# A hybrid attention and retention encoder layer on Trainium2: the gate's totals as split sums, the gate inside the last columns of w_out, and the last rows stored in six pieces

## The chip, the core and the metric

The kernel runs on one core of one Trainium2 chip. The metric is device time in microseconds (us): the median of three runs before the change is 965.22 us (965.08 to 965.33). Engines are named as in the profile: PE multiplies matrices, PEld is its weight load, DVE, ACT and POOL are the vector, scalar and GpSimd engines, SP is the engine that issues most DMA transfers. PE works on two kinds of fp32 here: plain fp32 (`F32`), and `fp32r` (`F32R`), a reduced form that it multiplies faster. The kernel keeps precision by splitting a value into a high part `hi`, rounded to fp32r, and a low part `lo`, the remainder, and by adding the products hi*hi, hi*lo and lo*hi.

## What is computed

One layer for 512 positions (`SEQ`) of width 2048 (`D_MODEL`), one batch. Cut to its core:

```python
def hybrid_layer(x, c_act, g, w_ada, b_ada, w_in, w_out, dec_f, dec_b):
    mod = c_act @ w_ada + b_ada
    shift, scale, gate = jnp.split(mod, 3, axis=-1)
    h = rms_norm(x, g) * (1.0 + scale[:, None]) + shift[:, None]
    proj = jnp.einsum('bsd,df->bsf', h, w_in)
    ...
    y = jnp.concatenate([y_a * jax.nn.silu(z_a), y_r * jax.nn.silu(z_r)], axis=-1)
    out = jnp.einsum('bsf,fd->bsd', y, w_out)
    return x + gate[:, None] * out

def reference(x, c, norm_gain, w_ada, b_ada, w_in, w_out, ret_decay_logit_f, ret_decay_logit_b, final_gain):
    c_act = jax.nn.silu(c)
    h = x
    for layer in range(DEPTH):
        h = hybrid_layer(h, c_act, norm_gain[layer], w_ada[layer], b_ada[layer], w_in[layer],
                         w_out[layer], ret_decay_logit_f[layer], ret_decay_logit_b[layer])
    return rms_norm(h, final_gain)
```

`DEPTH` is 1. `y_a` comes from eight attention heads, `y_r` from four retention heads, whose output is normalised per head. What matters here is the gate: a row of 2048 numbers, `c_act` times the last third of `w_ada` plus a bias. It multiplies each column of the output projection before `x` is added and the final norm is taken.

## The kernel before

**Projection and heads.** The weights `w_in` come by DMA into `raw` tiles. An *item* of a unit is 512 columns of such a tile: `conv` (line 166) splits it, ACT casting it to `whi` (line 173) and DVE subtracting for `wlo` (line 178), and `mm3` (lines 90 and 92) issues the three matmuls for each product. An item is 12 matmuls with 512 moving columns where the weights are the stationary side (units of q and k), and 24 with 256 where they are the moving side (v and z). `whi` and `wlo` have three buffers each (`WB`), and two items are split ahead of the one being multiplied (`LOOK`). Between items, `run_queue` issues what the heads have to do: scores, exponentials, `op` (the product with the values), and for retention a norm (POOL computes `rs`, DVE scales to `yn`) and transposes `tp` of `yn` (line 866). The accumulators of the projection are `pp`.

**The gate row.** `gate_pieces(h)` handles 512 columns of the gate, for h from 0 to 3: `load` brings 128 rows of `w_ada` into `graw`, `add` multiplies them by the entries of `c` on DVE and adds into `gacc` (128 x 512, line 1007), sixteen times. What is left is the sum over the 128 partitions: `total` (line 1015) takes a column of ones as the stationary side and `gacc` as the moving one, in fp32, so that row 0 of `psg` holds the sums; DVE adds the bias, and SP stores the row to `grow_d` in DRAM. All these pieces stand in the list `gate`, and `some_gate` takes one of them, at a rate of 0.9, each time an item of the later units is fed. Behind the sixteen additions of one h stand an empty entry and then `total`.

**The output projection.** `out_items` runs over column groups dg = 0, 1, 2 of 512 columns, then columns 1536 to 1791. For each, `finish` (line 1206) multiplies the accumulated `po` of a row tile by `gbc` (the gate row, read back from `grow_d` to all partitions, line 1209), adds it to the residual `res` (line 1210), sums the squares for the norm, and multiplies by the final gain `fbc` (line 1227). `columns(g)` issues the loads of `gbc`, `res` and `fbc` for a group. The last 256 columns are held back: during dg = 2 and the group behind it, `last_load` brings their weights and splits them into eight pairs of tiles `lhi` and `llo` (lines 1259 and 1260). At the very end, for each of the four row tiles, 48 matmuls with `lhi` and `llo` run, `finish` with slot 4 completes the row's sum of squares (`ms`) and its inverse root `rsf` (on POOL, line 1226), and `store` (line 1229) scales the 2048 columns by `rsf` and stores them in four pieces of 512.

**What sets the order.** The program is written in one thread, and each engine takes its instructions in an order that a scheduler makes out of it; waits between engines are semaphores. The side work (`sides`) is spread over the items of a column group by `run_items`.

Of the kernel before, what the change touches and what calls it, by code (L numbers as in the profile page):

```python
# [10 lines left out]
F32R = mybir.dt.float32r  # L11
I32 = mybir.dt.int32
AF = mybir.ActivationFunctionType
ALU = mybir.AluOpType
# [3 lines left out]
P = 128  # L18
D = 2048
S = 512  # L20
NT = S // P
NK = D // P
# [21 lines left out]
GR = 2  # L44
# [6 lines left out]
def trunk_kernel(ctx, tc, x, c, norm_gain, w_ada, b_ada, w_in, w_out, dec_f, dec_b, final_gain, out):  # L51
    nc = tc.nc
    x2, o2 = x[0], out[0]
    wi, wo, wa = w_in[0], w_out[0], w_ada[0]

    const = ctx.enter_context(tc.tile_pool(name="const", bufs=1))
# [6 lines left out]
    def bank(pool, nm):  # L63
        return pool.tile([P, 512], F32, tag="b", name=nm)
# [3 lines left out]
    def bank4(nm):  # L68
        turn[0] += 1
        return bank(psA if turn[0] % 4 else psM, nm)  # L70

    def f32(ap):
        return ap.bitcast(F32)
# [63 lines left out]
    make_identity(nc, ident)  # L137
    ones = const.tile([P, P], F32, name="ones")
    nc.gpsimd.memset(ones, 1.0)
    mhalf = const.tile([P, 4], F32, name="mhalf")  # L140
    nc.gpsimd.memset(mhalf, -0.5)
    mln2 = const.tile([P, 1], F32, name="mln2")
# [15 lines left out]
    def after(ins, ref):  # L158
        tc.add_manual_dep(
            ins.ins,  # L160
            ref.ins.name,
            mybir.DependencyInfo(mybir.DependencyClass.NoSync, mybir.DependencyReason.DATA),
            reason="after",
        )

    def conv(src, n, pin_low=None):
        hi = wp.tile([P, 512], F32R, tag="whi", name="whi", bufs=WB)
        lo = wp.tile([P, 512], F32R, tag="wlo", name="wlo", bufs=WB)
        dh, dl = hi[:, :n], lo[:, :n]
        if len(src.shape) == 3:  # L170
            dh = dh.rearrange("p (k f) -> p k f", k=src.shape[1])
            dl = dl.rearrange("p (k f) -> p k f", k=src.shape[1])
        c1 = nc.scalar.copy(dh, src)  # L173
        if pin_low is not None:
            pin_low.append(lambda: pin(nc.vector.tensor_tensor(dl, src, f32(dh), op=ALU.subtract)))
            pin(c1)
            return hi, lo
        c2 = nc.vector.tensor_tensor(dl, src, f32(dh), op=ALU.subtract)  # L178
        marks["conv"] = marks.get("conv", 0) + 1
        if marks["conv"] < 3:  # L180
            after(c1, marks["hh"])
            after(c2, marks["hl"])
        return hi, lo
# [739 lines left out]
    for ci, nk in enumerate(CHUNKS):  # L923
# [18 lines left out]
        for u in order:  # L942
# [22 lines left out]
            if u < N_PERSIST:  # L965
                pss = lambda u=u: persist[u]
                start, stop = ci == 0, lastc
            elif u in kept:
                pss = lambda u=u, kept=kept: kept[u]
                start, stop = False, u not in keep_now  # L970
            else:
                pss = lambda: [bank(psA, "pw") for _ in range(2)]
                start, stop = True, u not in keep_now
# [19 lines left out]
    def gate_pieces(h):  # L993
        st = {}
        gs = slice(2 * D + h * 512, 2 * D + (h + 1) * 512)

        def load(kr):
            raws[h * NK + kr] = pools["w"].tile([P, 512], F32, tag="graw", name="graw", bufs=GR)
            nc.sync.dma_start(raws[h * NK + kr], wa[kr * P : (kr + 1) * P, gs])

        def add(kr):
            raw = raws[h * NK + kr]
            if kr == 0:
                st["acc"] = pools["w"].tile([P, 512], F32, tag="gacc", name="gacc", bufs=1)
                nc.vector.tensor_scalar_mul(st["acc"], raw, ct[:, 0:1])
            else:
                nc.vector.scalar_tensor_tensor(  # L1007
                    st["acc"], raw, ct[:, kr : kr + 1], st["acc"], op0=ALU.mult, op1=ALU.add
                )

        def total():
            row = pools["w"].tile([1, 512], F32, tag="grow", name="grow", bufs=1)
            nc.sync.dma_start(row, b_ada[0:1, gs])
            ps = bank4("psg")[0:1, :]
            nc.tensor.matmul(ps, ones[:, 0:1], st["acc"], start=True, stop=True)
            nc.vector.tensor_tensor(row, row, ps, op=ALU.add)
            nc.sync.dma_start(grow_d[0:1, h * 512 : (h + 1) * 512], row)

        return load, add, total

    dramp = ctx.enter_context(tc.tile_pool(name="dramp", bufs=1, space=bass.MemoryType.DRAM))
    grow_d = dramp.tile([1, D], F32, name="grow_d")
    raws = {}
    gate = []
    gp = [gate_pieces(h) for h in range(4)]
    for n in range(4 * NK + GR):

        def step(n=n):
            if n >= GR:
                gp[(n - GR) // NK][1]((n - GR) % NK)  # L1030
            if n < 4 * NK:
                gp[n // NK][0](n % NK)

        gate.append(step)
        if n >= GR and (n - GR) % NK == NK - 1:
            gate.extend([None, gp[(n - GR) // NK][2]])
    gcount = [0]
    n_gate = len(gate)

# [101 lines left out]
    def ysplit(k):  # L1141
        nc.scalar.copy(yh[k], ytiles[k])
        nc.vector.tensor_tensor(yl[k], ytiles[k], f32(yh[k]), op=ALU.subtract)
# [14 lines left out]
    for k in range(NK):  # L1158
        hi = opA.tile([P, S], F32R, name=f"yh{k}")
        lo = opA.tile([P, S], F32R, name=f"yl{k}")  # L1160
# [27 lines left out]
    res = []  # L1188
# [3 lines left out]
    gbc = opB.tile([P, D], F32, name="gbc")  # L1192
    ssf = opB.tile([P, NT, 5], F32, name="ssf")
    sst = opB.tile([P, NT], F32, name="sst")
    rsf = opB.tile([P, NT], F32, name="rsf")

    def columns(g):
        cs = slice(g * 512, (g + 1) * 512)
        fg = final_gain.rearrange("(a d) -> a d", a=1)
        return (  # L1200
            [lambda: nc.sync.dma_start(gbc[:, cs], grow_d[0:1, cs].to_broadcast([P, 512]))]
            + [lambda t=t: nc.sync.dma_start(res[t][:, cs], x2[t * P : (t + 1) * P, cs]) for t in range(NT)]
            + [lambda: nc.sync.dma_start(fbc[:, cs], fg[0:1, cs].to_broadcast([P, 512]))]
        )

    def finish(t, c0, n, ps, slot):
        cs = slice(c0, c0 + n)
        tmp = opB.tile([P, 512], F32, tag="otmp", name="otmp", bufs=2)
        nc.vector.tensor_tensor(tmp[:, :n], ps, gbc[:, cs], op=ALU.mult)
        nc.vector.tensor_tensor(res[t][:, cs], res[t][:, cs], tmp[:, :n], op=ALU.add)  # L1210
        ss = ssf[:, t, slot : slot + 1]
        if slot < 4:
            nc.scalar.activation(tmp[:, :n], res[t][:, cs], AF.Square, accum_out=ss)
        else:
            nc.vector.tensor_tensor_reduce(
                tmp[:, :n], res[t][:, cs], res[t][:, cs], 1.0, 0.0, ALU.mult, ALU.add, ss
            )
        if slot == 3:
            nc.vector.reduce_sum(sst[:, t : t + 1], ssf[:, t, 0:4], axis=AX.X)
            nc.vector.tensor_scalar(sst[:, t : t + 1], sst[:, t : t + 1], 1.0 / D, EPS, op0=ALU.mult, op1=ALU.add)  # L1220
        if slot == 4:
            ms = small.tile([P, 4], F32, tag="ms", name="ms")
            nc.vector.scalar_tensor_tensor(
                ms[:, 0:1], ss, 1.0 / D, sst[:, t : t + 1], op0=ALU.mult, op1=ALU.add
            )
            nc.gpsimd.tensor_tensor(rsf[:, t : t + 1], ms[:, 0:1], mhalf[:, 0:1], op=ALU.pow)
        nc.vector.tensor_tensor(res[t][:, cs], res[t][:, cs], fbc[:, cs], op=ALU.mult)

    def store(t):
        for j in range(4):  # L1230
            v = res[t][:, j * 512 : (j + 1) * 512]
            if j == 1:
                nc.scalar.activation(v, v, AF.Copy, scale=rsf[:, t : t + 1])
            else:
                nc.vector.tensor_scalar_mul(v, v, rsf[:, t : t + 1])
            (nc.scalar if j % 2 else nc.sync).dma_start(o2[t * P : (t + 1) * P, j * 512 : (j + 1) * 512], v)

    def run_items(items, side):
        done = 0
        for n, it in enumerate(items):  # L1240
# [4 lines left out]
            done = upto  # L1245

    side = [lambda k=k: ysplit(k) for k in [*range(ny, NK), 0]] + columns(0)
    def last_load(k, i):
        if i == 0:
            raw = raw_tile()  # L1250
            nc.sync.dma_start(
                raw.rearrange("p (k f) -> p k f", k=4),
                wo[k * P : (k + 4) * P, 1792:2048].rearrange("(k p) f -> p k f", p=P),
            )
            hold_ll["raw"] = raw
        raw = hold_ll["raw"]
        hi = yp.tile([P, 512], F32R, tag="y", name="lhi")
        lo = yp.tile([P, 512], F32R, tag="y", name="llo")
        nc.scalar.copy(hi, raw[:, i * 512 : (i + 1) * 512])
        nc.vector.tensor_tensor(lo, raw[:, i * 512 : (i + 1) * 512], f32(hi), op=ALU.subtract)  # L1260
        keep.append((hi.rearrange("p (k f) -> p k f", k=2), lo.rearrange("p (k f) -> p k f", k=2)))

    keep = []
    hold_ll = {}
    ll = [lambda k=k, i=i: last_load(k, i) for k in range(0, NK, 4) for i in range(2)]
    sides = [side, columns(1) + columns(2), ll[:5] + columns(3), ll[5:]]
    run_items(g0[nf:], sides[0])
    for dg in (1, 2):
        own = (lambda nm: bank(psP, nm)) if dg == 2 else bank4
# [20 lines left out]
    for t in range(NT):  # L1290
        ts = slice(t * P, (t + 1) * P)
        ps = bank(psP, "po")[:, :256]
# [30 lines left out]
```

## Time and profile before

| | |
|---|---|
| median of three runs | 965.22 us (965.08 to 965.33) |
| the profiled execution | 967.67 us |
| its span, first to last instruction | 965.9 us |
| granted PE clock, mean | 0.995 |
| ACT busy | 376.0 us (39%) |
| POOL busy | 12.5 us (1%) |
| DMA | 141.49 MB, 146 GB/s over the span |

The page's second part divides the span into 40 slices and gives each engine's busy share in tenths:

```profile
PE   7999999999999999999999999999999999999996
DVE  4899998949777876665456565745534382545444
ACT  4742425253254655544343232422333272333321
```

PE is full in all but the first and the last slice; DVE is full at the start and half busy later. A row of the timeline gives the start in us, the duration, the engine, the line of the kernel, the operation and its tiles (output <- inputs), the shape, and a count where equal neighbours are put together; in brackets stands how long the engine was idle before it and what released it. Matmuls are pipelined: one starts before the modelled end of the one ahead, so the distance of two starts is what a matmul costs.

### The profile page before, as it was taken

The numbers are of one execution on the slowest core, as the hardware profiler recorded it, in microseconds if no ns is written. First come the engines' busy times: TensorE is split into PE (matmuls) and PEld (weight loads), VectorE is DVE, ScalarE is ACT, GpSimd is POOL, SyncE is SP. The second block draws the span as 40 slices with busy tenths as digits, with TensorE's granted clock in tenths as the row PEclk, the third lists the DMA queues.
The fourth block names the chain that finished last, engine by engine and source line by source line (L and its number), as shares of the span: only waits on it lengthen the run. The fifth ranks groups of instructions, "written<-read, shape, count | busy, mean of one in ns | idle before, by whom it ended". The sixth has DMA issues, their size and how long they took to land.

```text
span 965.9 us, 14382 instructions
## 1 busy us (share of the span) xinstructions
PE 945.4 (98%) x5602; PEld 821.6 (85%) x5602; DVE 614.0 (64%) x1076; ACT 376.0 (39%) x738; POOL 12.5 (1%) x25
## 2 busy tenths in 40 slices
PE   7999999999999999999999999999999999999996
PEld 6787688788888888988997899988899988888896
DVE  4899998949777876665456565745534382545444
ACT  4742425253254655544343232422333272333321
POOL 2000000000000000000000000000000000000001
PEclk9999999999999999999999999999999999999998
DMA  9997798424642222112225515436322147243304
GB/s 329 333 296 239 262 314 289 162 89 128 198 154 66 87 66 66 55 55 88 67 66 175 196 57 190 147 90 202 101 67 89 66 162 274 90 128 131 110 1 174
DMA packets 108947, 141.49 MB, mean 146 GB/s; under 512 B 5656, under 2 KB 78024, under 8 KB 108496
## 3 DMA queue, kind: packets, MB, share of 16 engines
q1 hardware_dynamic: 107200, 135.83, 43.5%
q10 hardware_dynamic: 1584, 4.72, 1.3%
q8 instruction: 44, 0.72, 0.3%
q14 instruction: 23, 0.19, 0.1%
q0 software_dynamic: 96, 0.03, 0.0%
HBM read 136.36 MB, written 4.20 MB: 146 GB/s over the span
## 4 chain that ended last, share of the span: by engine, by line
PE 82%; DMA 7%; DVE 6%; issue 2%; SPq 1%; ACT 1%; POOL 0%; POOLq 0%; DVEq 0%; ACTq 0%
PE pp L92 24%; PE pp L90 12%; PE po L92 12%; PE pw L92 11%; PE po L90 6%; PE pw L90 6%; PE op L92 3%; DMA araw<-in_w_ada_dram 3%; PE sp L92 2%; DMA graw<-in_w_ada_dram 2%; DVE aacc L234 2%; PE op L90 2%; PE tp L782 1%; DVE wlo L178 1%; SPq L117 1%
## 5 line engine op out<-in xcount | busy, mean ns | idle before, releaser
L173 ACT CAST whi<-raw 128x512 fp32r<-128x512 f32 (+1 forms) x289 | 175.1, 606 | 433.5 <-PE pp L92 203.1
L178 DVE TENSOR_TENSOR wlo<-raw,whi 128x512 fp32r<-128x512 f32 (+1 forms) x288 | 193.5, 672 | 208.3 <-ACT whi L173 201.8
L92 PE MATMUL pp<-wlo,hh 128*128 128x256 f32 x576 | 162.3, 282 | 0.5 <-DVE wlo L178 0.4
L90 PE MATMUL pp<-whi,hh 128*128 128x256 f32 x576 | 162.6, 282 | 0.0
L92 PE MATMUL pp<-whi,hl 128*128 128x256 f32 x576 | 161.6, 281 | 0.0
L90 PEld LDWEIGHTS pp<-whi,hh 128*128 128x128 f32 x576 | 108.5, 188 | 2.5 <-ACT sc L851 1.7
L92 PEld LDWEIGHTS pp<-wlo,hh 128*128 128x128 f32 x576 | 108.6, 189 | 1.9 <-DVE wlo L178 0.9
L92 PEld LDWEIGHTS pp<-whi,hl 128*128 128x128 f32 x576 | 108.6, 188 | 0.0
L90 PE MATMUL pw<-hh,whi 128*128 128x512 f32 x256 | 103.5, 404 | 3.6 <-ACT acc L952 1.9
L92 PE MATMUL pw<-hh,wlo 128*128 128x512 f32 x256 | 102.3, 400 | 0.8 <-DVE wlo L178 0.8
L90 PE MATMUL pp<-hh,whi 128*128 128x512 f32 x256 | 102.0, 398 | 0.4 <-DVE kl L682 0.4
L92 PE MATMUL pw<-hl,whi 128*128 128x512 f32 x256 | 102.0, 398 | 0.0
L92 PE MATMUL pp<-hh,wlo 128*128 128x512 f32 x256 | 101.2, 397 | 0.0
L92 PE MATMUL pp<-hl,whi 128*128 128x512 f32 x256 | 101.2, 395 | 0.0
L92 PE MATMUL po<-wlo,yh 128*128 128x512 f32 (+1 forms) x252 | 92.7, 368 | 0.0
L92 PE MATMUL po<-whi,yl 128*128 128x512 f32 (+1 forms) x252 | 92.6, 368 | 0.0
L90 PE MATMUL po<-whi,yh 128*128 128x512 f32 (+1 forms) x252 | 92.6, 367 | 0.0
L234 DVE SCALAR_TENSOR_TENSOR aacc<-araw,ct,aacc 128x512 f32<-128x512 f32 (+2 forms) x75 | 76.0, 1015 | 6.7 <-ACT aacc L230 3.8
L954 DVE TENSOR_TENSOR acc<-acc,pw 128x512 f32<-128x512 f32 x100 | 67.0, 684 | 8.0 <-PE pw L92 7.6
L1007 DVE SCALAR_TENSOR_TENSOR gacc<-graw,ct,gacc 128x512 f32<-128x512 f32 x60 | 45.0, 750 | 40.9 <-DMA graw<-in_w_ada_dram 40.7
L90 PEld LDWEIGHTS pw<-hh,whi 128*128 128x128 f32 x256 | 48.5, 190 | 19.1 <-DVE acc L954 4.9
L90 PEld LDWEIGHTS pp<-hh,whi 128*128 128x128 f32 x256 | 48.1, 188 | 13.4 <-ACT e L727 0.9
(234 smaller groups left out, 1559.3 us busy)
## 6 DMA issues: line engine op xcount, KB each, us to landing
raw<-in_w_in_dram SPq DMA_DIRECT2D x94, 512.0 KB, 3.7
araw<-in_w_ada_dram SPq DMA_DIRECT2D x48, 512.0 KB, 6.7
graw<-in_w_ada_dram SPq DMA_DIRECT2D x64, 256.0 KB, 2.9
raw<-in_w_out_dram SPq DMA_DIRECT2D x32, 512.0 KB, 3.7
raw<-in_w_in_dram SPq DMA_DIRECT2D x16, 384.0 KB, 4.2
araw<-in_w_ada_dram SPq DMA_DIRECT2D x16, 384.0 KB, 4.9
res<-in_x_dram SPq DMA_DIRECT2D x16, 256.0 KB, 6.2
raw<-in_w_in_dram SPq DMA_DIRECT2D x11, 256.0 KB, 5.8
```

Source lines behind the costliest of these rows:

```text
L90: nc.tensor.matmul(o, lh, rh, start=start, stop=False, skip_group_check=True)
L92: nc.tensor.matmul(o, a, b, start=False, stop=stop and b is (rl if swap else rh), skip_group_check=True)
L117: q.dma_start(raw0[b][:, i * 8 : (i + 1) * 8], wa[i * 8 * P : (i + 1) * 8 * P, b * D : b * D + P].rearrange("(a p) f -> p a f", p=P),)
L173: c1 = nc.scalar.copy(dh, src)
L178: c2 = nc.vector.tensor_tensor(dl, src, f32(dh), op=ALU.subtract)
L234: ins = nc.vector.scalar_tensor_tensor(acc[:, :, :n], rv[:, a], ct[:, kr + a : kr + a + 1], acc[:, :, :n], op0=ALU.mult, op1=ALU.add,)
L782: nc.tensor.transpose(tp_[:, j * P : (j + 1) * P], pt[:, j * P : (j + 1) * P], ident)
L954: nc.vector.tensor_tensor(accs[u][i], accs[u][i], ps[i], op=ALU.add)
L1007: nc.vector.scalar_tensor_tensor(st["acc"], raw, ct[:, kr : kr + 1], st["acc"], op0=ALU.mult, op1=ALU.add)
```

## The change

Three parts, in the diff below. First, `parts` splits `gacc` by the same `conv` that splits weights, so in one of its three pairs of buffers, and `total` sums both halves with two fp32r matmuls over `ones_r`, a 128 x 1 column of ones cast once at the start. `parts` is a new entry of the list `gate` in the place that `total` had, and `total` follows one item behind. Second, the gate goes into the last 256 columns of `w_out`: `last_load` multiplies the raw weights in place by `gbc` (line 1275 of the new kernel), 256 columns at a time, before they are split, and `finish` with slot 4 has no product with the gate. The row of `gbc` for those columns is loaded at the end of the side work of dg = 1. Third, `store` works in six pieces of 256, 384, 384, 384, 320 and 320 columns; ACT scales the second and the fifth and issues the fifth, SP issues the other five.

```diff
--- before.py
+++ after.py
@@ -137,6 +137,7 @@
     make_identity(nc, ident)
     ones = const.tile([P, P], F32, name="ones")
     nc.gpsimd.memset(ones, 1.0)
+    ones_r = const.tile([P, 1], F32R, name="ones_r")
     mhalf = const.tile([P, 4], F32, name="mhalf")
     nc.gpsimd.memset(mhalf, -0.5)
     mln2 = const.tile([P, 1], F32, name="mln2")
@@ -1008,18 +1009,23 @@
                     st["acc"], raw, ct[:, kr : kr + 1], st["acc"], op0=ALU.mult, op1=ALU.add
                 )
 
+        def parts():
+            st["parts"] = conv(st["acc"], 512)
+
         def total():
             row = pools["w"].tile([1, 512], F32, tag="grow", name="grow", bufs=1)
             nc.sync.dma_start(row, b_ada[0:1, gs])
             ps = bank4("psg")[0:1, :]
-            nc.tensor.matmul(ps, ones[:, 0:1], st["acc"], start=True, stop=True)
+            for i in range(2):
+                nc.tensor.matmul(ps, ones_r, st["parts"][i], start=i == 0, stop=i == 1)
             nc.vector.tensor_tensor(row, row, ps, op=ALU.add)
             nc.sync.dma_start(grow_d[0:1, h * 512 : (h + 1) * 512], row)
 
-        return load, add, total
+        return load, add, parts, total
 
     dramp = ctx.enter_context(tc.tile_pool(name="dramp", bufs=1, space=bass.MemoryType.DRAM))
     grow_d = dramp.tile([1, D], F32, name="grow_d")
+    nc.scalar.copy(ones_r, ones[:, 0:1])
     raws = {}
     gate = []
     gp = [gate_pieces(h) for h in range(4)]
@@ -1033,7 +1039,7 @@
 
         gate.append(step)
         if n >= GR and (n - GR) % NK == NK - 1:
-            gate.extend([None, gp[(n - GR) // NK][2]])
+            gate.extend([None, gp[(n - GR) // NK][2], gp[(n - GR) // NK][3]])
     gcount = [0]
     n_gate = len(gate)
 
@@ -1194,11 +1200,15 @@
     sst = opB.tile([P, NT], F32, name="sst")
     rsf = opB.tile([P, NT], F32, name="rsf")
 
+    def gate_row(s):
+        nc.sync.dma_start(gbc[:, s], grow_d[0:1, s].to_broadcast([P, s.stop - s.start]))
+
     def columns(g):
         cs = slice(g * 512, (g + 1) * 512)
+        gs = slice(g * 512, 1792 if g == 3 else (g + 1) * 512)
         fg = final_gain.rearrange("(a d) -> a d", a=1)
         return (
-            [lambda: nc.sync.dma_start(gbc[:, cs], grow_d[0:1, cs].to_broadcast([P, 512]))]
+            [lambda: gate_row(gs)]
             + [lambda t=t: nc.sync.dma_start(res[t][:, cs], x2[t * P : (t + 1) * P, cs]) for t in range(NT)]
             + [lambda: nc.sync.dma_start(fbc[:, cs], fg[0:1, cs].to_broadcast([P, 512]))]
         )
@@ -1206,8 +1216,10 @@
     def finish(t, c0, n, ps, slot):
         cs = slice(c0, c0 + n)
         tmp = opB.tile([P, 512], F32, tag="otmp", name="otmp", bufs=2)
-        nc.vector.tensor_tensor(tmp[:, :n], ps, gbc[:, cs], op=ALU.mult)
-        nc.vector.tensor_tensor(res[t][:, cs], res[t][:, cs], tmp[:, :n], op=ALU.add)
+        if slot < 4:
+            nc.vector.tensor_tensor(tmp[:, :n], ps, gbc[:, cs], op=ALU.mult)
+            ps = tmp[:, :n]
+        nc.vector.tensor_tensor(res[t][:, cs], res[t][:, cs], ps, op=ALU.add)
         ss = ssf[:, t, slot : slot + 1]
         if slot < 4:
             nc.scalar.activation(tmp[:, :n], res[t][:, cs], AF.Square, accum_out=ss)
@@ -1227,13 +1239,14 @@
         nc.vector.tensor_tensor(res[t][:, cs], res[t][:, cs], fbc[:, cs], op=ALU.mult)
 
     def store(t):
-        for j in range(4):
-            v = res[t][:, j * 512 : (j + 1) * 512]
-            if j == 1:
+        cuts = (0, 256, 640, 1024, 1408, 1728, D)
+        for i in range(6):
+            v = res[t][:, cuts[i] : cuts[i + 1]]
+            if i in (1, 4):
                 nc.scalar.activation(v, v, AF.Copy, scale=rsf[:, t : t + 1])
             else:
                 nc.vector.tensor_scalar_mul(v, v, rsf[:, t : t + 1])
-            (nc.scalar if j % 2 else nc.sync).dma_start(o2[t * P : (t + 1) * P, j * 512 : (j + 1) * 512], v)
+            (nc.scalar if i == 4 else nc.sync).dma_start(o2[t * P : (t + 1) * P, cuts[i] : cuts[i + 1]], v)
 
     def run_items(items, side):
         done = 0
@@ -1256,14 +1269,18 @@
         raw = hold_ll["raw"]
         hi = yp.tile([P, 512], F32R, tag="y", name="lhi")
         lo = yp.tile([P, 512], F32R, tag="y", name="llo")
-        nc.scalar.copy(hi, raw[:, i * 512 : (i + 1) * 512])
-        nc.vector.tensor_tensor(lo, raw[:, i * 512 : (i + 1) * 512], f32(hi), op=ALU.subtract)
+        w = raw[:, i * 512 : (i + 1) * 512]
+        for j in range(2):
+            v = w[:, j * 256 : (j + 1) * 256]
+            nc.vector.tensor_tensor(v, v, gbc[:, 1792:2048], op=ALU.mult)
+        nc.scalar.copy(hi, w)
+        nc.vector.tensor_tensor(lo, w, f32(hi), op=ALU.subtract)
         keep.append((hi.rearrange("p (k f) -> p k f", k=2), lo.rearrange("p (k f) -> p k f", k=2)))
 
     keep = []
     hold_ll = {}
     ll = [lambda k=k, i=i: last_load(k, i) for k in range(0, NK, 4) for i in range(2)]
-    sides = [side, columns(1) + columns(2), ll[:5] + columns(3), ll[5:]]
+    sides = [side, columns(1) + columns(2) + [lambda: gate_row(slice(1792, D))], ll[:5] + columns(3), ll[5:]]
     run_items(g0[nf:], sides[0])
     for dg in (1, 2):
         own = (lambda nm: bank(psP, nm)) if dg == 2 else bank4
```

The new lines move instructions on the engines at three places.

**PE, at the second total.** The names: `op` is the product of retention head 0, `pp` with `whi` and `wlo` the projection items behind it. Before:

```order
L90 MATMUL op<-vh_5040,pth 128x256
L92 MATMUL op<-vl_5042,pth 128x256
L92 MATMUL op<-vh_5040,ptl 128x256
L1015 MATMUL psg<-gacc,ones 1x512
L90 MATMUL pp<-whi,hh_85 128x256
L92 MATMUL pp<-wlo,hh_85 128x256
L92 MATMUL pp<-whi,hl_1731 128x256
```

After, at the same place, the projection items follow the `op` matmuls directly:

```order
L90 MATMUL op<-vh_5042,pth 128x256
L92 MATMUL op<-vl_5044,pth 128x256
L92 MATMUL op<-vh_5042,ptl 128x256
L90 MATMUL pp<-whi,hh_85 128x256
L92 MATMUL pp<-wlo,hh_85 128x256
L92 MATMUL pp<-whi,hl_1732 128x256
```

and the total stands further on:

```order
L92 MATMUL pp<-whi,hl_1732 128x256
L90 MATMUL pp<-whi,hh_88 128x256
L92 MATMUL pp<-wlo,hh_88 128x256
L92 MATMUL pp<-whi,hl_1732 128x256
L1020 MATMUL psg<-whi,ones_r 1x512
L1020 MATMUL psg<-wlo,ones_r 1x512
L90 MATMUL pp<-whi,hh_89 128x256
L92 MATMUL pp<-wlo,hh_89 128x256
```

The total moved past two rounds of 24 projection matmuls and the eight transposes `tp` between them, and is two matmuls now. The other three totals moved back by one, three and four items.

**ACT, at the first total.** Here `g` and `e` belong to the gating by SiLU of the first retention unit, and `whi<-raw` is the split of weights. Before:

```order
L725 ACTIVATE g_5105<-pp,mln_137 128x512
L726 ACTIVATE e<-pp 128x512
L727 ACTIVATE e<-e 128x512
L725 ACTIVATE g_5112<-pp,mln_137 128x512
L173 CAST whi<-raw 128x512
L726 ACTIVATE e<-pp 128x512
L727 ACTIVATE e<-e 128x512
L173 CAST whi<-raw 128x512 x7
```

After:

```order
L726 ACTIVATE g_5107<-pp,mln_138 128x512
L727 ACTIVATE e<-pp 128x512
L728 ACTIVATE e<-e 128x512
L726 ACTIVATE g_5114<-pp,mln_138 128x512
L174 CAST whi<-gacc 128x512
L727 ACTIVATE e<-pp 128x512
L728 ACTIVATE e<-e 128x512
L174 CAST whi<-raw 128x512 x8
```

The cast of `gacc` took the place of a weight cast, and that weight cast stands with the others behind the two exponentials.

**DVE, in the output projection.** The place is the end of group dg = 1, when `finish` runs for its four row tiles (lines 1209, 1210, 1227 before; 1220, 1222, 1239 after) while the first pieces of the last columns are split (`llo`) along with the weights of the running group (`wlo`). Before:

```order
L1227 TENSOR_TENSOR res_7877<-res_7877,fbc 128x512
L1209 TENSOR_TENSOR otmp<-po,gbc 128x512 x2
L1210 TENSOR_TENSOR res_7878<-res_7878,otmp 128x512
L178 TENSOR_TENSOR wlo<-raw,whi 128x512
L1210 TENSOR_TENSOR res_7879<-res_7879,otmp 128x512
L1227 TENSOR_TENSOR res_7878<-res_7878,fbc 128x512
L1260 TENSOR_TENSOR llo<-raw,lhi 128x512
L1227 TENSOR_TENSOR res_7879<-res_7879,fbc 128x512
L178 TENSOR_TENSOR wlo<-raw,whi 128x512
L1209 TENSOR_TENSOR otmp<-po,gbc 128x512
L1260 TENSOR_TENSOR llo<-raw,lhi 128x512
```

After:

```order
L1277 TENSOR_TENSOR llo<-raw,lhi 128x512
L1239 TENSOR_TENSOR res_7899<-res_7899,fbc 128x512
L1220 TENSOR_TENSOR otmp<-po,gbc 128x512
L179 TENSOR_TENSOR wlo<-raw,whi 128x512
L1222 TENSOR_TENSOR res_7900<-res_7900,otmp 128x512
L1220 TENSOR_TENSOR otmp<-po,gbc 128x512
L1222 TENSOR_TENSOR res_7901<-res_7901,otmp 128x512
L1275 TENSOR_TENSOR raw<-raw,gbc 128x256 x2
L1239 TENSOR_TENSOR res_7900<-res_7900,fbc 128x512
L1239 TENSOR_TENSOR res_7901<-res_7901,fbc 128x512
L1277 TENSOR_TENSOR llo<-raw,lhi 128x512
L179 TENSOR_TENSOR wlo<-raw,whi 128x512
```

The multiplications of `raw` by `gbc` (line 1275) stand between the rows of `finish`, ahead of the `llo` that needs them, and the `llo` and `wlo` behind them moved back by as many rows.

## The prediction

> **What bounds the kernel now.** First the page's busy shares, then the waits of PE in the stretch 232 to 957 us, behind the opening phase and up to the last matmul.
>
> ```profile
> PE 945.4 (98%) x5602; PEld 821.6 (85%) x5602; DVE 614.0 (64%) x1076; ACT 376.0 (39%) x738; POOL 12.5 (1%) x25
> ```
> ```profile
> PE pp L92 <- DVE wlo L178: 0.4, 1, 0.4
> PE pp L90 <- DVE kl L682: 0.4, 1, 0.4
> ```
>
> PE works nearly all the time, and in 725 us it is seen to wait twice, 0.8 us in all. So up to 957 us the time is the matmuls themselves: an edit counts by the PE time it removes or adds, and by a wait that it makes. Behind the last matmul (957.39) PE is out, and what counts is the chain from there to the last stored byte. The profiled execution took 967.67 us (span 965.9); the sum is made against it and set off against the median, 965.22.
>
> **Gate totals: what goes.** PE's timeline at the first of four totals, and the group of all four:
>
> ```profile
> 507.64 0.28 PE L92 MATMUL pp<-wlo,hh 128*128 128x256 f32 x1
> 507.76 0.28 PE L92 MATMUL pp<-whi,hl 128*128 128x256 f32 x1
> 507.96 1.02 PE L1015 MATMUL psg<-gacc,ones 128*1 128x512 f32 x2
> 508.91 0.49 PE L90 MATMUL pp<-hh,whi 128*128 128x512 f32 x1
> 509.48 0.40 PE L92 MATMUL pp<-hl,whi 128*128 128x512 f32 x1
> 511.35 0.39 PE L92 MATMUL pp<-hl,whi 128*128 128x512 f32 x1
> ```
> ```profile
> L1015 PE MATMUL psg<-gacc,ones x8: 590/591/592, 508.0 to 709.6; 128*1 128x512 f32 x8
> ```
>
> The first number of a row is its start; starts give the pace, since matmuls overlap. A 256-column fp32r matmul starts 0.12 behind the one before (507.64, 507.76). From 509.48 to 511.35 stand eight steps of 512 columns, 0.234 each. From 507.76 to 509.48 there is one step of 256 and two of 512, 0.12 + 0.47 = 0.59 of 1.72 us; the other **1.13 us is the fp32 total**, including its slow start and the stretched matmul behind it. The two fp32r matmuls that replace it have 512 moving columns each. No row shows an fp32r matmul with one output column. The nearest rows are the fp32r ones above, 0.234, and the fp32 total, 1.13; I take 2 x 0.234 = 0.47, since the type is the same and the columns that stream are as many, and keep 1.13 each as the upper end. A total so saves 0.66 to 0.67.
>
> [...]
>
> **The second total also covered a wait.** It stood between the last `op` matmul of retention head 0 and two projection items, into which the transposes `tp` of that head are mixed. Head 1 has the same sequence with no total:
>
> ```profile
> 573.41 0.28 PE L92 MATMUL op<-vh,ptl 128*128 128x256 f32 x1
> 573.62 1.02 PE L1015 MATMUL psg<-gacc,ones 128*1 128x512 f32 x2
> 574.57 0.39 PE L90 MATMUL pp<-whi,hh 128*128 128x256 f32 x1
> 581.36 0.28 PE L90 MATMUL pp<-whi,hh 128*128 128x256 f32 x1
> ```
> ```profile
> 630.68 0.28 PE L92 MATMUL op<-vx,ptl 128*128 128x256 f32 x1
> 633.76 0.83 PE L866 MATMUL tp<-ident,yn 128*128 128x128 f32 x4
> 637.72 0.28 PE L90 MATMUL pp<-whi,hh 128*128 128x256 f32 x1
> ```
> ```profile
> 633.76 0.20 PEld L866 LDWEIGHTS tp<-ident,yn 128*128 128x128 f32 x2 [0.19 <-DVE yn L862]
> ```
>
> From the last `op` to the second item behind (581.36; 637.72 in head 1) it takes 7.95 us with the total and 7.04 without, where the weight load of `tp` waits for `yn`, 0.19 twice. So only 0.91 of the 1.13 goes here: 0.91 - 0.47 = 0.44. The other totals stand beside no such chain. **Sum of the totals: 3 x 0.67 + 0.44 = 2.45 us.**
>
> **What must stay covered.** Each total now first needs a cast of `gacc` on ACT and a subtraction on DVE. It comes as one more item in the row of weight splits and holds one of three pairs of buffers until its matmuls are done; splits of the weights then run one item ahead of PE, not two.
>
> ```profile
> 508.98 0.61 ACT L173 CAST whi<-raw 128x512 fp32r<-128x512 f32 x1
> ```
> ```profile
> L178 DVE TENSOR_TENSOR wlo<-raw,whi 128x512 fp32r<-128x512 f32 (+1 forms) x288 | 193.5, 672 | 208.3 <-ACT whi L173 201.8
> ```
> ```profile
> ACT whi L173 <- PE pp L92: 166.9, 89, 5.0
> ```
>
> The split is 0.61 + 0.67 = 1.3 us, 1.7 with a DVE instruction ahead of it; an item lasts 12 x 0.234 = 2.8 us. ACT's casts waited 166.9 us for PE to free buffers, so there is room. Tightest is the first total: the cast of `gacc` takes the slot of the row at 508.98, the subtraction ends about 510.3, and PE comes to the total one item behind 507.88, at 510.7: 0.4 us to spare. The others have more matmuls in front. I take 0; a miss costs 0.4 or so each, 1 us in all.
>
> **The gate in the last columns' weights.** Sixteen multiplications of 256 columns go to DVE, two ahead of each `lhi` cast, at 0.42 each by the like row L1227, 6.7 us; one product of 256 columns leaves each of the four row tiles.
>
> ```profile
> L1227 DVE TENSOR_TENSOR res<-res,fbc 128x256 f32<-128x256 f32 x8 | 3.3, 417 | 0.0
> ```
> ```profile
> 868.68 0.37 SPq L1251 DMA_DIRECT2D raw<-in_w_out_dram  x1
> 873.16 0.62 ACT L1259 CAST lhi<-raw 128x512 fp32r<-128x512 f32 x1 [0.75 <-DMA raw<-in_w_out_dram]
> 874.44 0.69 DVE L1227 TENSOR_TENSOR res<-res,fbc 128x512 f32<-128x512 f32 x1
> 875.05 0.68 DVE L178 TENSOR_TENSOR wlo<-raw,whi 128x512 fp32r<-128x512 f32 x1
> 878.63 0.39 PE L90 MATMUL po<-whi,yh 128*128 128x512 f32 x1
> ```
>
> They lie beside 92 us of output projection, but in bunches. The tight place is around 870, where `finish` of a column group, two `last_load` pieces and the weight splits share DVE. The split at 875.05 serves the item that PE starts at 878.63: it ends at 875.73, 2.9 us early. After, the load for the third pair of pieces waits longer: its buffer is free only when the second `llo` before it is done, at about 870.8 by the new order on DVE, some 2.1 us later than 868.68. With 4.5 us from there to the data's use (873.16), 875.3, two multiplications (0.7), and two products with `fbc`, `llo` and `wlo` at 0.6 apiece (874.44 to 875.05), the wanted `wlo` ends near 878.4, 0.2 to 0.3 us before PE. I take 0, and up to 1.0 if it is late. What is queued behind a late multiplication on DVE is the next `wlo`, and PE waits for that.
>
> **The tail.** The timeline, the groups, the store's own line and the DMA windows:
>
> ```profile
> 957.71 0.42 DVE L1209 TENSOR_TENSOR otmp<-po,gbc 128x256 f32<-128x256 f32 x1 [2.05 <-PE po L92]
> 958.16 0.42 DVE L1210 TENSOR_TENSOR res<-res,otmp 128x256 f32<-128x256 f32 x1
> 959.33 0.66 POOL L1226 TENSOR_TENSOR rsf<-ms,mhalf 128x1 f32<-128x1 f32 x1 [4.99 <-DVE ms L1223]
> 960.03 0.72 ACT L1233 ACTIVATE res<-res,rsf 128x512 f32<-128x512 f32 x1 [4.93 <-POOL rsf L1226]
> 960.03 1.28 DVE L1235 TENSOR_SCALAR res<-res,rsf 128x512 f32<-128x512 f32 x3 [0.44 <-POOL rsf L1226]
> 960.54 0.81 SPq L1236 DMA_DIRECT2D out_dram<-res  x2
> ```
> ```profile
> L1235 DVE TENSOR_SCALAR res<-res,rsf 128x512 f32<-128x512 f32 x12 | 5.1, 483 | 1.9 <-POOL rsf L1226 1.9
> L355 DVE TENSOR_SCALAR xt<-xt,rsx 128x128 f32<-128x128 f32 x4 | 1.1, 283 | 0.8 <-POOL rsx L351 0.7
> ```
> ```profile
> L1236 SPq DMA_DIRECT2D out_dram<-res x8: 332/366/424, 943.7 to 961.0; - x8
> ```
> ```profile
> 962.00:963.00 1.00, 0.00 (x0) 0.00 (x0) 0.00 (x0) 0.00 (x0) 0.00 (x0) 0.50 0.98 373
> 963.00:964.00 1.00, 0.00 (x0) 0.00 (x0) 0.00 (x0) 0.00 (x0) 0.00 (x0) 0.50 1.02 381
> 964.00:965.00 1.00, 0.00 (x0) 0.00 (x0) 0.00 (x0) 0.00 (x0) 0.00 (x0) 0.50 0.16 57
> ```
>
> The product goes, and the sum reads PSUM itself: 958.16 - 957.71 = **0.45 us**, on the chain to `rsf` and so to the end. Then the store: 1.05 MB leave at some 380 GB/s (the last two columns: share of the DMA engines, GB/s), so the end is the first byte's start plus 2.8 us, as long as pieces are issued fast enough. The first piece has 256 columns in place of 512; its scaling lies between 0.283 (128) and 0.483 (512), 0.35, so its issue comes **0.13 us** earlier. SP issues five pieces at about 0.40 (0.81 for two): 0.40 us at 380 GB/s is 152 KB. The first piece has 131 KB, and SP is 0.06 late behind it; the others have 164 to 196 KB, and SP gets ahead. ACT's first piece (384 columns, under 0.72) is ready before SP comes to it, 0.4 behind the first. Last issue at 1.6 us behind the first, while the data still run: the gain stands. Tail 0.58, between 0.25 (C below) and 0.75 (a start 0.3 earlier, should the small first piece flow at once).
>
> **Sum.** 2.45 + 0.58 = 3.03: 967.67 becomes 964.6, and by the median 965.22 - 3.03 = **962.2 us**.
>
> **Rivals.**
>
> *B, covers torn:* the totals save 2.45, but late splits or DVE around 870 give back 1 to 2 us: 963.2 to 964.2. For it: the margins of 0.3 and 0.4 above; against it: DVE at 64% and ACT's 166.9 us of waiting for PE. 0.17.
>
> *C, store bound by issues:* pieces of 1 to 1.5 KB per partition cannot fill the DMA engines, and the six take longer than the four. If the rate fell from 380 to 340 GB/s, 1.05 MB would take 3.08 for 2.76 us, 0.3 more: tail 0.58 - 0.32 = 0.26, time 962.5. For it: SP's pitch, five issues instead of two; against it: 152 KB per pitch, above. [...] The windows of before (pieces of 2 KB per partition, 373 to 381) can't decide it. 0.13.
>
> *D, slower:* an fp32r matmul with one output column is no faster than fp32. Then each total is two of the old price. With m for one matmul, the change is 8m - 4 x 1.13 + 0.22 - 0.58 (the 0.22 is the wait that the second total covered): at m = 1.13 it gives +4.2, 969.4. It is slower by 0.2% from m = 0.85 on, and within 0.2% from 0.37. [...] This is also the case in which the change does not do what it says. 0.04.
>
> **How the numbers follow.** Forecast 0.66 (961.7 to 962.9), B 0.17, C 0.13, D 0.04. 0.2% of 965.2 is 1.9 us, about what a measurement of this kernel can tell from no change: faster means under 963.3. The forecast and C lie under it, as does a fifth of B: 0.66 + 0.13 + 0.03 = 0.82. Four fifths of B, 0.14, lie within, D above or within: slower 0.03, same 0.15. The range goes from 961.6 (tail 0.75, totals 2.85 if nothing of the covered wait shows and starts are smoother) to 963.8, which takes in C, the forecast and half of B.
>
> **What would show it.** PE's timeline at each total: two matmuls whose starts lie 0.23 apart and no stretched one behind; 1.1 apart would be D. `tp` of head 0 waits 0.2 for `yn`. In PE's waits, rows on `wlo`, `whi` or `psg` above 0.5 in sum would be B, and their times say whether it is a total or 870 to 880. In the tail, the sum at PE's end + 0.3 with no product, the first issue some 0.6 nearer to PE's end, and windows at 370 to 380 GB/s; under 350, or gaps between issues, would be C. A median above 963.3 proves the sum wrong.

## The result and the profile after

The changed kernel takes 953.26 us (median of six, 951.5 to 954.4) against 965.28 before: a ratio of 0.9871, with a 95% interval from 0.9857 to 0.9886. That is **12 us less, four times the 3.0 that was forecast**, and 8 us below the range. The profiled execution after took 951.88 us (span 950.1).

The page's busy line, to be set beside that of before:

```profile
PE 928.7 (98%) x5602; PEld 812.3 (85%) x5602; DVE 619.6 (65%) x1096; ACT 379.0 (40%) x747; POOL 12.5 (1%) x25
```

PE ran as many matmuls as before (5602 in both) and was busy 16.7 us less (945.4 before; the two profiled executions lie 15.8 us apart). No edit takes out that much work, so the step from one matmul to the next must have become shorter. The waits of PE, 225 to 945 us:

```profile
PE pp L92 <- DVE wlo L179: 0.5, 1, 0.5
PE pp L90 <- DVE kl L683: 0.4, 1, 0.4
PE tp L867 <- DVE yn L863: 0.4, 1, 0.4
PE pw L90 <- DVE acc L955: 0.2, 1, 0.2
```

The row of note that is new is the wait for `yn`. It is not the one that the second total used to cover: it lies in the transposes of the last retention head, among matmuls of the output projection, where nothing was forecast. The wait that was forecast shows in the weight loads of head 0 alone, 0.30 and 0.19 for twice 0.19. First the row of the last head, then those of head 0:

```profile
764.22 0.44 PE L867 MATMUL tp<-ident,yn 128*128 128x128 f32 x2 [0.39 <-DVE yn L863]
```
```profile
566.22 0.20 PEld L867 LDWEIGHTS tp<-ident,yn 128*128 128x128 f32 x2 [0.30 <-DVE yn L863]
566.61 0.20 PEld L867 LDWEIGHTS tp<-ident,yn 128*128 128x128 f32 x2 [0.19 <-DVE yn L863]
```

The first total after, in PE's timeline:

```profile
501.65 0.39 PE L92 MATMUL pp<-hl,whi 128*128 128x512 f32 x1
501.88 0.40 PE L92 MATMUL pp<-hh,wlo 128*128 128x512 f32 x1
502.12 0.40 PE L1020 MATMUL psg<-whi,ones_r 128*1 128x512 f32 x1
502.35 0.40 PE L1020 MATMUL psg<-wlo,ones_r 128*1 128x512 f32 x1
502.59 0.39 PE L90 MATMUL pp<-hh,whi 128*128 128x512 f32 x1
```

The two matmuls cost 0.47 us (502.12 to 502.59), with no stretched one behind, just as in the sum. So the totals are not where 12 us came from. The same 48 projection matmuls, which no edit touches, first before, then after (PE's timeline, first and last row of the stretch):

```profile
520.21 0.40 PE L90 MATMUL pp<-hh,whi 128*128 128x512 f32 x1
531.41 0.40 PE L90 MATMUL pp<-hh,whi 128*128 128x512 f32 x1
```
```profile
510.84 0.39 PE L90 MATMUL pp<-hh,whi 128*128 128x512 f32 x1
521.83 0.39 PE L90 MATMUL pp<-hh,whi 128*128 128x512 f32 x1
```

11.20 us before, 10.99 after: 0.2333 and 0.2289 us a step, for the same operands with no wait. To the nanosecond the stretch takes 11.200 and 10.986. Matmuls of 256 columns go from 0.118 to 0.113. **In such stretches a projection matmul costs about 4.4 ns less, whether it streams 512 columns or 256**, and this begins some 35 us after the start, over 450 us ahead of the first total. It isn't so everywhere: the output projection has 0.233, 0.234 before, `op` 0.118 in both, and part of the projection's 256-column stretches stay at 0.118.

The tail did not do what was forecast either. Its timeline after, from the last matmul, with SP's rows one by one, then the DMA windows:

```profile
941.59 0.28 PE L92 MATMUL po<-lhi,yl 128*128 128x256 f32 x1
941.91 0.42 DVE L1222 TENSOR_TENSOR res<-res,po 128x256 f32<-128x256 f32 x1 [2.59 <-PE po L92]
943.07 0.66 POOL L1238 TENSOR_TENSOR rsf<-ms,mhalf 128x1 f32<-128x1 f32 x1 [5.09 <-DVE ms L1235]
943.77 1.31 DVE L1248 TENSOR_SCALAR res<-res,rsf 128x256 f32<-128x256 f32 x4 [0.44 <-POOL rsf L1238]
944.15 0.33 SPq L1249 DMA_DIRECT2D out_dram<-res  x1
...
945.08 0.37 SPq L1249 DMA_DIRECT2D out_dram<-res  x1
945.56 0.39 SPq L1249 DMA_DIRECT2D out_dram<-res  x1
946.37 0.33 SPq L1249 DMA_DIRECT2D out_dram<-res  x1
```
```profile
946.00:947.00 1.00, 0.00 (x0) 0.00 (x0) 0.00 (x0) 0.00 (x0) 0.00 (x0) 0.50 1.00 361
947.00:948.00 1.00, 0.00 (x0) 0.00 (x0) 0.00 (x0) 0.00 (x0) 0.00 (x0) 0.50 0.99 359
```

The first store is issued 2.56 us behind PE's last matmul (944.15 - 941.59), 3.15 before: 0.59 earlier, as forecast. But the span ends 8.51 behind it in both (950.1 - 941.59, 965.9 - 957.39). SP's issues lie 0.5 apart and the fifth 0.81 behind the fourth, at 4.78 and not 4.16; the DMA engines move 360 GB/s, not 380.

### The profile page after: what moved, and what is told of

Same layout as the page of the kernel before. It is cut to its first block, busy times and chain, and to the rows that moved or that the text cites. A ratio compares the mean times of both kernels' runs of the same rounds, so it can differ in the third digit from the quotient of the medians.

```text
span 950.1 us, 14445 instructions
## 1 busy us (share of the span) xinstructions
PE 928.7 (98%) x5602; PEld 812.3 (85%) x5602; DVE 619.6 (65%) x1096; ACT 379.0 (40%) x747; POOL 12.5 (1%) x25
## 4 chain that ended last, share of the span: by engine, by line
PE 81%; DVE 6%; DMA 6%; ACT 2%; issue 2%; SPq 1%; POOL 0%; POOLq 0%; DVEq 0%; ACTq 0%
PE pp L92 23%; PE po L92 12%; PE pp L90 12%; PE pw L92 12%; PE po L90 6%; PE pw L90 6%; PE op L92 3%; DMA graw<-in_w_ada_dram 2%; DMA araw<-in_w_ada_dram 2%; PE sp L92 2%; PE op L90 2%; PE tp L783 1%; DVE wlo L179 1%; DVE aacc L235 1%; SPq L117 1%
```

## The experiments

Two questions: what made untouched matmuls faster, and what ate the tail's 0.59 us? The first clue is what the change does to memory. `ones_r` is allocated among the constants and takes a slot of 32 bytes per partition; every tile that is allocated behind it on the left side stands 32 bytes further on: `raw`, `whi`, `wlo`, the tiles of the heads, `res`. `hh`, `hl`, `yh` and `yl` are allocated from the right side and stay. Before, in the built program, `whi` and `wlo` start at a multiple of 64 bytes and `hh`, `hl` at a multiple plus 32; after, both at a multiple plus 32. (These addresses are the built program's; no trace shows them. The traces show what a shift by 32 or 64 bytes does.) Theory 1: this placement sets the pace. Theory 2: the new instructions and their order do. Theory 3: the executions merely differ.

**Placement alone, and the change without it.** One line for each kernel: in `before_pad32` and `before_pad64` a tile that nothing uses, of 32 or 64 bytes, in the place of `ones_r`; in `after_pad32` 32 bytes more behind `ones_r`; in `after_unshifted` `ones_r` in spare bytes of `mhalf`.

```diff
 # before_pad32 (before_pad64: [P, 16]; after_pad32: the same line in the changed kernel)
+    const.tile([P, 8], F32, name="pad")
     mhalf = const.tile([P, 4], F32, name="mhalf")
```
```diff
 # after_unshifted, against the changed kernel
-    ones_r = const.tile([P, 1], F32R, name="ones_r")
-    mhalf = const.tile([P, 4], F32, name="mhalf")
-    nc.gpsimd.memset(mhalf, -0.5)
+    mhalf = const.tile([P, 8], F32, name="mhalf")
+    ones_r = mhalf[:, 4:5].bitcast(F32R)
+    nc.gpsimd.memset(mhalf[:, 0:4], -0.5)
```

> The kernel before with one unused tile of 32 bytes per partition in the constants' pool, in the place where the change puts ones_r; no instruction differs. Theory 1 (placement: ones_r moves every tile behind it in on-chip memory by 32 bytes, and the pace of the matmuls hangs on that): 953 to 957 us, steps of 0.229 us for 512 columns and 0.113 for 256 in most units, as in the profile after. Theory 2 (the pace follows from the changed instructions, their order or their time): 965, steps of 0.233 and 0.118 as before. Theory 3 (the executions differ for a reason outside the kernel): either, without relation to the pad.

> The kernel before with an unused tile of 64 bytes per partition in the same place. Theory 1, if only the position within 64 bytes counts: 965, as before. If any shift helps: 953 to 957. Theory 2: 965.

> The changed kernel with a further unused 32 bytes behind ones_r, so that all later tiles stand 64 bytes behind their places of before. Theory 1, position within 64 bytes: the pace of before returns, and only the sum of the prediction's terms is left, 961 to 963 us. Theory 2: 953.

> The changed kernel with ones_r in spare bytes of the tile mhalf, so that no other tile moves; the instructions are the same. Theory 1: 962.2 us, 3.0 less than before, the prediction's terms alone, with steps of 0.233 and 0.118. Theory 2: 953, as after.

Measured, with the time of those 48 matmuls in each trace:

| kernel | median us | before, same chip | ratio, 95% interval | 48 matmuls, us |
|---|---|---|---|---|
| before_pad32 | 957.94 | 966.19 | 0.991 [0.9893, 0.9928] | 10.986 |
| before_pad64 | 964.98 | 966.19 | 0.9985 [0.9976, 0.9993] | 11.200 |
| after_pad32 | 963.5 | 966.19 | 0.9973 [0.9962, 0.9984] | 11.199 |
| after_unshifted | 964.02 | 966.19 | 0.9971 [0.9961, 0.9981] | 11.200 |

An unused tile of 32 bytes makes the kernel before 8 us faster, and no instruction differs; 64 bytes do nearly nothing. (The two kernels with `pad32` stand 0.9 and 0.5 us above what was expected of them, on a chip whose kernel before is 0.9 slower than in the section on the result.) The other way round, the changed kernel with its tiles in their old places gains 0.29% (2.8 us by the ratio, 1.8 to 3.8 by its interval; 2.2 between the medians). Theories 2 and 3 fall: the pace follows the bytes in four of four kernels. Its first and last row of the 48 in `before_pad32`:

```profile
513.40 0.39 PE L90 MATMUL pp<-hh,whi 128*128 128x512 f32 x1
524.38 0.39 PE L90 MATMUL pp<-hh,whi 128*128 128x512 f32 x1
```

**Which tiles, and against what?** Only the distance of two operands, or their own place? `before_right32` moves the right side's pools by 32 bytes (a pool of one unused tile opened ahead of `hp`), `before_both32` moves both sides, `before_wp32` moves the weights' pool by 32 and every left-side pool behind it by 64.

```diff
 # before_right32; before_both32 has this and the pad of before_pad32
+    rpad = ctx.enter_context(tc.tile_pool(name="rpad", bufs=1, side="right"))
+    rpad.tile([P, 8], F32, name="padr")
     hp_scope = ExitStack()
```
```diff
 # before_wp32: the pad of before_pad32, and behind the weights' pool
     small = ctx.enter_context(tc.tile_pool(name="small", bufs=8))
+    small.tile([P, 8], F32, name="pads", bufs=1)
```

> The kernel before with 32 unused bytes per partition ahead of the pools on the right side of on-chip memory: hh, hl, yh and yl move by 32 bytes, whi and wlo stay. If the two operands of a matmul must stand alike within 64 bytes (theory 1a, relative): whi at 0 and hh at 0, so the fast steps of 0.229 and 0.113 in the projection, 955 to 959 us. If whi and wlo must stand at 32 (theory 1b, absolute): 965.

> The kernel before with 32 bytes on either side: whi and wlo at 32 within 64 bytes, hh and hl at 0. Theory 1a: they differ again, so the slow steps, 965 us. Theory 1b: 955 to 959.

> The kernel before with 32 bytes ahead of the pool of raw, whi and wlo and 32 behind it, so that all pools behind it (y, the heads' tiles, res) move by 64. If the weights' place against hh and hl is what counts: 955 to 959, as with the pad of 32. If another tile's place does it (those of the heads, of the accumulators, or the engines that write them): 965.

| `whi`, `wlo` within 64 bytes | `hh`, `hl` | kernel | median us | ratio to before | 48 matmuls, us |
|---|---|---|---|---|---|
| 0 | 32 | before | 965.32 | 1 | 11.200 |
| 32 | 32 | before_wp32 | 957.67 | 0.9917 [0.9892, 0.9941] | 10.987 |
| 0 | 0 | before_right32 | 956.06 | 0.9901 [0.9876, 0.9926] | 10.986 |
| 32 | 0 | before_both32 | 965.16 | 0.9998 [0.9984, 1.0011] | 11.200 |

Theory 1a holds and 1b falls: it is the place of the two operands of a matmul **relative to each other**. Alike within 64 bytes, the fast step is there; 32 bytes apart, it is not, in this stretch in all four cells. `before_wp32` shows that the weights against `hh` and `hl` suffice; the tiles of the heads and of `y` keep their places within 64 bytes in it. (`raw` moves with `whi` and `wlo`, but no matmul of the stretch reads it.) First and last row in `before_right32`, then in `before_both32`:

```profile
514.03 0.39 PE L90 MATMUL pp<-hh,whi 128*128 128x512 f32 x1
525.01 0.39 PE L90 MATMUL pp<-hh,whi 128*128 128x512 f32 x1
```
```profile
518.69 0.39 PE L90 MATMUL pp<-hh,whi 128*128 128x512 f32 x1
529.89 0.39 PE L90 MATMUL pp<-hh,whi 128*128 128x512 f32 x1
```

**The tail: six pieces or four?** `after_store4` is the changed kernel with the old `store`; `after_six_alternate` keeps the six pieces and lets SP and ACT issue in turn; `after_five` has pieces of 256, 512, 512, 512, 256.

```diff
 # after_six_alternate
-            (nc.scalar if i == 4 else nc.sync).dma_start(...)
+            (nc.scalar if i % 2 else nc.sync).dma_start(...)
 # after_five: that line, and
-        cuts = (0, 256, 640, 1024, 1408, 1728, D)
-        for i in range(6):
+        cuts = (0, 256, 768, 1280, 1792, D)
+        for i in range(5):
...
-            if i in (1, 4):
+            if i == 1:
```

> The changed kernel with the four pieces of 512 columns of before in store. In the profile after, the last bytes land 7.53 us behind PE's last matmul, 7.47 before, though the first store is issued 0.59 earlier. If the six pieces eat the gain: landing at about 7.0 behind PE's end, 0.5 us less than the changed kernel, 952.8. If the end is set by something else: 7.5, 953.3.

> The changed kernel, its six pieces issued in turn by SP and ACT. If SP's five issues in a row are what makes the six pieces slow: the last bytes land 7.0 to 7.1 us behind PE's end, 7.55 in the changed kernel. If it is the pieces' width (1 to 1.5 KB per partition): still 7.4 or more.

> The changed kernel with five pieces of 256, 512, 512, 512 and 256 columns, issued in turn by SP and ACT. If narrow pieces move slower: between, 7.0 to 7.2 behind PE's end, since three of five are 2 KB per partition. If only SP's queue counts: about 6.9, the first piece's lead over the four-piece store kept whole.

| kernel | median us | ratio to before, same chip | first issue behind PE's end | last landing behind it | end of the span behind it |
|---|---|---|---|---|---|
| before | 965.28 | 1 | 3.15 | 7.47 | 8.50 |
| changed | 953.26 | 0.9871 [0.9857, 0.9886] | 2.56 | 7.55 | 8.52 |
| after_store4 | 951.99 | 0.9857 [0.9834, 0.988] | 2.70 | 7.01 | 7.97 |
| after_six_alternate | 953.18 | 0.9862 [0.9844, 0.9879] | 2.56 | 7.10 | 8.06 |
| after_five | 951.34 | 0.9848 [0.9829, 0.9866] | 2.56 | 6.94 | 8.15 |

(A landing is the last update that a store's transfer makes on its semaphore in the trace; PE's end is the start of its last matmul.) Six pieces issued in turn land 0.45 earlier than six issued mostly by SP: it is SP's five issues in a row, not the width of the pieces, that eats most of the gain. The figures are steady: the fifth issue lies at 4.77 to 4.80 and the last landing at 7.52 to 7.55 in the three traces with the changed `store`, and the landing at 6.98 to 7.01 in the three with the four old pieces in the changed kernel. The stores of `after_six_alternate`, three to a queue, and of `after_five`:

```profile
945.60 1.31 SPq L1249 DMA_DIRECT2D out_dram<-res  x3
945.87 1.53 ACTq L1249 DMA_DIRECT2D out_dram<-res  x3
```
```profile
944.10 1.38 SPq L1249 DMA_DIRECT2D out_dram<-res  x3
944.47 0.86 ACTq L1249 DMA_DIRECT2D out_dram<-res  x2
```

Width may cost something too: 7.10 with six pieces of 1 to 1.5 KB per partition against 6.94 with five, three of them of 2 KB; but 6.94 is also what was expected if SP's queue alone counted, and number and width weren't changed apart. Nor does the earlier landing shorten the run: the span of `after_five` ends 0.09 behind that of `after_six_alternate`, for in its trace SP goes through five further semaphores behind the last landing, some 0.06 us apiece, and through one or two in the others. By the span's end the four old pieces are the best of these. The intervals of these kernels' ratios overlap, so the traces carry the verdict on 0.1 to 0.5 us.

**Everything alike?** `after_aligned4` adds to `after_store4` the pad in `small` and makes `dec` 64 bytes wide, so that by the built program's addresses each fp32r operand, of the heads and of the last columns too, starts at a multiple of 64 plus 32.

```diff
+    small.tile([P, 8], F32, name="pads", bufs=1)
...
-            dec = pools["w"].tile([P, 8], F32, name="dec")
+            dec = pools["w"].tile([P, 16], F32, name="dec")[:, 0:8]
```

> The changed kernel with the four-piece store, and with 32 unused bytes in two places, so that every operand of the fp32r matmuls stands at 32 within 64 bytes: those of the heads (pth stood at 0, vh at 32), of the last columns (lhi and llo at 0, yh at 32). If alike placement is what allows the fast steps: the last row tiles go from 0.120 to 0.118 or 0.113, 0.4 to 1.3 us less in 192 matmuls, and op from 0.118 towards 0.113, at most 2 us; 949 to 951.5. If the matmuls of the heads and of the last columns are slow for another reason: 952, as with four pieces alone.

It took 954.15 us (0.9879 [0.986, 0.9897]), where `after_store4` had 0.9857, with intervals that overlap: no gain, and this expectation failed. The last columns kept 0.120 a step, and `op` stayed at 0.118. So **alike placement permits the fast step and does not assure it**.

**The forecast's terms alone.** `after_unshifted_store4` is `after_unshifted` with the old `store`: only the totals and the gate in the last columns are left of the change.

> The changed kernel with ones_r in spare bytes of mhalf (no tile moves) and with the four-piece store of before: only the totals and the gate in the last columns are left of the change. If the forecast's terms hold (totals 2.45, the product in the tail 0.45) and placement was all that was missed: 2.9 us less than before, slow steps of 0.233, last bytes 7.0 us behind PE's end. If the totals or the tail give less without the moved tiles: 1.5 us less or nothing.

962.29 us against 966.19, 0.9966 [0.9954, 0.9977], 3.3 us by the ratio (2.2 to 4.4) where 2.9 were forecast; the last bytes land 6.98 behind PE's end.

## Why the prediction was wrong

**The step that failed** is in the first part: "up to 957 us the time is the matmuls themselves: an edit counts by the PE time it removes or adds, and by a wait that it makes". It took the step of a matmul, 0.234 and 0.12, for a constant of the kernel. The step hangs on where the operands stand, and the diff moved some of them: one new tile, of one column, among the constants. The changed kernel and `after_unshifted` have the same instructions; by their ratios to before (0.9871, 0.9971) 9.7 us lie between them. In their traces the same stretch, from one matmul of the late projection to another, shows it. First the changed kernel, then the unshifted one, then before:

```profile
491.77 0.28 PE L92 MATMUL pp<-whi,hl 128*128 128x256 f32 x1
...
754.02 0.28 PE L90 MATMUL pp<-whi,hh 128*128 128x256 f32 x1
```
```profile
497.19 0.28 PE L92 MATMUL pp<-whi,hl 128*128 128x256 f32 x1
...
764.17 0.28 PE L90 MATMUL pp<-whi,hh 128*128 128x256 f32 x1
```
```profile
500.01 0.28 PE L92 MATMUL pp<-whi,hl 128*128 128x256 f32 x1
...
770.04 0.28 PE L90 MATMUL pp<-whi,hh 128*128 128x256 f32 x1
```

262.25, 266.98 and 270.03 us: placement is worth some 4.7 here alone. From before to unshifted it is 3.05, and all four totals lie in it. Taken one by one, from a matmul ahead of each total to one behind its new place, they save 0.68, 0.41, 0.67 and 0.67: **2.43 us, where 2.45 were forecast**. The other 0.6 lies between the second and the third total, 582 to 643 us before, where matmuls wait for a late `wlo`. The longest such wait in each, before and then unshifted:

```profile
605.27 0.39 PE L92 MATMUL pp<-wlo,hh 128*128 128x256 f32 x1 [0.41 <-DVE wlo L178]
```
```profile
615.01 0.38 PE L92 MATMUL pp<-wlo,hh 128*128 128x256 f32 x1 [0.41 <-DVE wlo L179]
```

Before, more matmuls nearby start late for the same reason, 1.3 us in all; unshifted has 0.7. This stretch takes 61.2, 60.2 and 62.0 us in `before`, `before_pad64` and `before_both32`, which differ in no instruction and have the slow step, so the 0.6 can't be credited to the change. No rival had the placement, and the range had no room for it.

**The other steps.** The fp32r matmul with one output column costs 0.235 where 0.234 was taken; rival D falls. The second total's cover was worth what head 1 showed (0.41 saved, 0.44 forecast). The covers that were weighed held: in PE's waits there is none for a split of `gacc` and none between 860 and 880, so rival B falls, and the thin margins of 0.2 to 0.4 sufficed. One that nobody weighed didn't: in the transposes of the last retention head the weight load waits 0.79 to 0.83 us for `yn`, 0.45 before, and that stretch of PE is 0.35 us longer in `after_unshifted`. Why `yn` comes late there was not followed up. The product's 0.45 is gone from the chain (the scaling starts 2.18 behind PE's end, 2.64 before).

**The tail's second half was wrong:** "the others have 164 to 196 KB, and SP gets ahead". The price of an issue on SP was taken as 0.40, from two issues in a row; with five it was 0.43 to 0.50 and the last 0.81. So 0.58 became nothing, and rival C was nearer, though it blamed the rate: 360 for 380 GB/s is 0.15 us in 1.05 MB, and the late last issue did most of the rest (the 0.45 that issuing in turn gives back). What held up the fifth issue is not shown; its data had been scaled 1.3 us before (945.08).

No run shows a fall to the 340 GB/s of rival C: the full windows have 359 to 361 GB/s for pieces of 1 to 1.5 KB per partition, in the changed kernel, and 373 to 381 for 2 KB, before, a loss of some 5%.

Set together, by the ratios to before: 2.8 us without the moved tiles and 9.7 for placement, 12.5 in all, and 12.0 between the medians. The placement's 9.7 is net of a loss of 0.4 in the last row tiles, whose 192 matmuls take 22.92 us in the changed kernel and 22.50 before and unshifted. That `after_unshifted` gains nearly the 3.0 of the forecast is in part luck: its terms come to 2.43 for the totals, 0.35 lost at `yn` and nothing in the tail, about 2.1, inside its interval of 1.8 to 3.8.

## What to carry to other kernels

Where PE is full, look at the start-to-start step of matmuls that an edit doesn't touch before crediting the edit: a difference of 2 to 4% there (0.2333 to 0.2289 us, 0.1178 to 0.1133), at the same granted clock of 1.00, was placement here, and a kernel with an unused tile of the same size told it apart (`before_pad32`, 8 us). In a kernel bound by matmuls, try to place the two operands alike within 64 bytes, with a pad of 32 on either side, and measure: here it permitted the fast step, no more (`after_aligned4` kept 0.120 in the last columns). At the end of a kernel, price a store's pieces by the issues that stand in a row on one queue: here six pieces landed 0.45 us later with SP issuing five of them than with SP and ACT in turn.

## What the runs showed that was not expected

The step of an fp32r matmul of the projection has two values here, 0.2289 and 0.2333 us at 512 columns, about 0.1133 and 0.1178 at 256; the difference is some 4.4 ns at both widths, not a share. The granted clock was 1.00 in both kernels from 200 to 900 us, so it does not explain the difference.

Where the operands stand alike, nearly every stretch of 24 matmuls is either wholly fast or wholly slow (of 82 with 256 columns and no step over 0.15 us in the changed kernel's projection, 61 have 0.1133 to 0.1145 a step and 21 have 0.1177 to 0.1180), and which it is differs from kernel to kernel: the 512-column groups of the output projection stayed at 0.233 to 0.234 in every run, though by the built program's addresses `whi` and `yh` stood alike in several, but columns 1536 to 1791 ran at 0.113 in `before_wp32` alone. What switches it is open. `before_pad32` spread from 955.0 to 959.1 us in four executions, so the switching may differ between executions too; no run here settles that. The lowest median was that of `after_five`, 951.34 us, but it is not clear of `after_store4` with 951.99.
